# Retention in three bursts, its read-out turned by VectorE and a trip to DRAM

## The chip, the cores and the metric

The kernel runs on one core of a Trainium2 chip. The metric is the device time of one execution in microseconds (us). A core has five engines with a queue of instructions each, worked off in order: TensorE (PE in the profile, with its weight loads as PEld), VectorE (DVE), ScalarE (ACT), GpSimd (POOL) and SyncE (SP, which here only issues transfers). ACT and POOL issue transfers too. An instruction waits in its queue for semaphores that others raise, and whatever stands behind it waits as well.

## The reference, cut to what matters

Two layers, 512 positions, 1024 channels, float32. Each layer has a token mixer with three parallel branches (RWKV-7, retention, a gated spatial unit), merged by sigmoid gates, and then a gated MLP.

```python
p_rw, p_ret, p_sg, gate_logits = jnp.split(h @ w_in[l], in_cuts, axis=-1)
y_rw, y_ret, y_sg = rwkv7_branch(p_rw, ...), retention_branch(p_ret, cos, sin), sgu_branch(p_sg, ...)
proj = jnp.einsum('bsgc,gcd->bsgd', jnp.stack([y_rw, y_ret, y_sg], axis=2), w_branch[l])
x = x + jnp.sum(jax.nn.sigmoid(gate_logits...) * proj, axis=2) @ w_out[l]

# retention_branch: 4 chunks of 128 positions, 4 heads, q and k of 64, v of 128 channels
scores = jnp.einsum('bhnid,bhnjd->bhnij', qc, kc) * decay_in
inner = jnp.einsum('bhnij,bhnje->bhnie', scores, vc)
cross = jnp.einsum('bhnid,nbhde,hi->bhnie', qc, R_prev, q_dec)     # R_prev: running states
y = inner + cross
y = y * lax.rsqrt(jnp.mean(y * y, axis=-1, keepdims=True) + EPS)
return y.reshape(B, S, RET_V_WIDTH) * jax.nn.silu(g)
```

## The kernel before

Activations are kept with channels on the partitions (128) and positions along the row (512). A product is made of float32r halves: a raw weight tile of 128x512 (`wr`, three buffers) is loaded by SP (L123), cast on ACT to a high half (`sh` or `wh`, L136), the remainder is made on VectorE (`sl` or `wl`, L137), and for each 128 input channels TensorE does three wide matmuls (L153) into a PSUM accumulator (`acc`, four buffers). A raw buffer is free once its `sl` is made. `unit` works ahead by a few tiles. The inputs of a product are split in the same way by `split` (`hi` on ACT L145, `lo` on VectorE L146).

A scheduler sets the order inside each engine's queue from the order of the code; what is marked `keep_in_program_order` (called `po`) isn't moved against other marked instructions of its engine. What is shown below as the order of a queue is its result.

The string `SEQ` writes out the second half of the mixer, a letter a step:
- `0`, `1`, `2`: one of the eight merges of a branch (0 RWKV, 1 retention, 2 spatial gating). `merge` loads the gate (`gth`, issued by POOL) that an earlier stage left in DRAM, makes a product of four weight blocks (12 wide matmuls), multiplies gate and accumulator on VectorE and adds it to the sum.
- `H`: `ret_heads` loads the turned queries and keys (`qF`, `kF`) and copies halves of them and of the values to the other half of the partitions (`qS`, `vs`).
- `G`: `sgu_out`, a group of the spatial gating: four matmuls of 128x128 and two VectorE passes (`sgm`), then `split`. `U`: one block of its first factor.
- `S`: `ret_row(read, score)`, a burst of small matmuls of the retention. Five of them: the first makes the scores of chunk 0, the next three read chunk 0, 1, 2 out and make the scores of the next chunk, the last reads chunk 3. Two call `ret_states` (running states `R`). A read-out gives `X` in PSUM, with positions on the partitions. ACT squares it and sums (`rsq`, `rss`), VectorE multiplies by the gate (in place of `vt`, the tile `yg`), POOL raises the mean to -0.5 (`rrr`), ACT scales by that.
- `Y`: `ret_out` turns the four scaled tiles to channels on the partitions, by 16 TensorE transposes into PSUM and a `split` from there.

`to_dram` is an older helper: VectorE transposes within 32x32 blocks, and four transfers of 64 KB put the blocks in place in a DRAM tile (`tn`), in pieces of 128 bytes. The RWKV read-out and the queries and keys go this way, issued by POOL. Tiles come from pools: `u` (31 buffers of 128x512), `r` (16), `f` (39), `sm` (four PSUM banks).

## Time and profile before

| what | value |
|---|---|
| time, three runs | 1702.79, 1702.88, 1703.18 us; median 1702.88 |
| the profiled execution | 1702.28 us; span 1700.6 us; granted TensorE clock 0.999 |
| wide matmuls of the weights x hi/lo halves (the three groups `sh`, `sl`) | 432.3, 431.6, 431.1 us busy |
| ACT's cast of weights, VectorE's remainder (`sh`, `sl`) | 235.1 us, 263.4 us busy |
| TensorE's 32 transposes (16 a layer) | 271 to 273 ns each, between 407.0 and 1252.5 us |
| transfers | 214.20 MB, mean 126 GB/s |

The span is the time from the first to the last instruction of the profiled execution. A row of a timeline gives the start, the duration, engine, line, operation, output and inputs, shapes and the count of what was merged into the row; in brackets stands the idle time ahead of it and who ended that. Matmuls are pipelined, so the distance of two starts is the cost, not the duration. A float32 matmul of small tiles shows as two records.

### The profile page before, as it was taken

Reading aid. Unit: us, or ns where it says so; the run is one execution under the profiler, and the core shown is the slowest. Engines: PE = TensorE matmul, PEld = TensorE weight load, DVE = VectorE, ACT = ScalarE, POOL = GpSimd, SP = SyncE. Lnnn points to the kernel's source line nnn. Section 1 sums busy time; section 2 is a strip of 40 time slices with the busy share of each in tenths; the row PEclk is TensorE's granted clock in tenths of the full one; section 3 lists DMA queues with packets and bytes.
Section 4 is the critical chain, followed back from the end, with each engine's and each line's share of the span. In section 5 each row is a group of like instructions: output and inputs, shape, how many; then the busy total and the mean of one; then the engine's idle time right before and its main releaser. Section 6 shows DMA issues by size and latency. Waiting matters only on the chain.

```text
span 1700.6 us, 28356 instructions
## 1 busy us (share of the span) xinstructions
PE 1692.3 (100%) x10564; PEld 1390.6 (82%) x10564; DVE 1141.6 (67%) x2032; ACT 765.9 (45%) x1341; POOL 245.4 (14%) x326
## 2 busy tenths in 40 slices
PE   9999999999999999999999999999999999999998
PEld 7888877888888888888888888778888888888887
DVE  7887856567569777653367786564765798876432
ACT  7564433535355444333255634345343554443322
POOL 1122235114100000000011203441141000000010
PEclk9999999999999999999999999999999999999999
DMA  5334566446443333243332346555364454432531
GB/s 175 91 101 151 147 151 152 141 130 194 137 149 100 96 97 99 69 119 110 115 113 80 112 142 155 148 141 161 108 210 141 132 138 123 124 107 68 155 100 55
DMA packets 151337, 214.20 MB, mean 126 GB/s; under 512 B 48416, under 2 KB 57248, under 8 KB 151200
## 3 DMA queue, kind: packets, MB, share of 16 engines
q1 hardware_dynamic: 129552, 171.62, 34.2%
q0 software_dynamic: 9600, 21.77, 4.9%
q10 hardware_dynamic: 12048, 19.00, 3.4%
q8 instruction: 83, 1.36, 0.3%
q14 instruction: 54, 0.44, 0.1%
HBM read 181.92 MB, written 23.07 MB: 121 GB/s over the span
## 4 chain that ended last, share of the span: by engine, by line
PE 99%; DMA 0%; ACT 0%; DVE 0%; issue 0%
PE acc L153 88%; PE sm L153 4%; PE sm L647 2%; PE acc L287 1%; PE sm L561 1%; PE sm L915 1%; PE acc L1009 0%; PE sm L524 0%; PE sm L523 0%; DMA g<-pcols 0%; PE sm L898 0%; PE sm L959 0%; PE sm L805 0%; PE sm L795 0%; PE sm L578 0%; PE sm L579 0%
## 5 line engine op out<-in xcount | busy, mean ns | idle before, releaser
L153 PE MATMUL acc<-lo,sh 128*128 128x512 f32 x1108 | 432.3, 390 | 0.0
L153 PE MATMUL acc<-hi,sh 128*128 128x512 f32 x1108 | 431.6, 390 | 0.0
L153 PE MATMUL acc<-hi,sl 128*128 128x512 f32 x1108 | 431.1, 389 | 0.0
L136 ACT CAST sh<-wr 128x512 fp32r<-128x512 f32 (+1 forms) x385 | 235.1, 615 | 380.2 <-PE acc L153 263.4
L137 DVE TENSOR_TENSOR sl<-wr,sh 128x512 fp32r<-128x512 f32 (+1 forms) x385 | 263.4, 687 | 170.5 <-ACT sh L136 104.8
L153 PEld LDWEIGHTS acc<-lo,sh 128*128 128x128 f32 x1108 | 208.0, 188 | 44.1 <-issue 0.7
L153 PEld LDWEIGHTS acc<-hi,sl 128*128 128x128 f32 x1108 | 208.0, 188 | 43.7 <-issue 0.3
L153 PEld LDWEIGHTS acc<-hi,sh 128*128 128x128 f32 x1108 | 208.0, 188 | 42.9 <-issue 0.2
L136 ACT CAST wh<-wr 128x512 fp32r<-128x512 f32 x194 | 120.2, 620 | 227.9 <-PE acc L153 209.2
L153 PE MATMUL acc<-lo,wh 128*128 128x512 f32 x556 | 219.4, 395 | 0.0
L153 PE MATMUL acc<-hi,wl 128*128 128x512 f32 x556 | 217.0, 390 | 0.0
L153 PE MATMUL acc<-hi,wh 128*128 128x512 f32 x556 | 216.6, 390 | 0.0
L137 DVE TENSOR_TENSOR wl<-wr,wh 128x512 fp32r<-128x512 f32 x195 | 138.9, 712 | 111.6 <-ACT wh L136 104.7
L153 PEld LDWEIGHTS acc<-hi,wl 128*128 128x128 f32 x556 | 104.4, 188 | 22.6 <-issue 0.7
L153 PEld LDWEIGHTS acc<-lo,wh 128*128 128x128 f32 x556 | 104.3, 188 | 22.6 <-issue 0.3
L153 PEld LDWEIGHTS acc<-hi,wh 128*128 128x128 f32 x556 | 104.4, 188 | 20.9
L153 PE MATMUL acc<-ah,sh 128*128 128x512 f32 x352 | 108.3, 389 | 0.0
L1077 DVE TENSOR_TENSOR fu<-acc,rsF 128x512 f32<-128x512 f32 x88 | 60.5, 689 | 62.3 <-PE acc L153 62.3
L1079 ACT ACTIVATE cv<-fu,pc 128x512 f32<-128x512 f32 x88 | 71.6, 816 | 50.4 <-DVE fu L1077 47.5
L153 PE MATMUL acc<-wl,hi 128*128 128x512 f32 x192 | 78.0, 406 | 0.0
L1080 DVE SCALAR_TENSOR_TENSOR cv<-fu,pc,cv 128x511 f32<-128x511 f32 x88 | 65.4, 746 | 18.6 <-ACT cv L1079 18.6
L153 PEld LDWEIGHTS acc<-ah,sh 128*128 128x128 f32 x352 | 66.1, 188 | 13.7
(335 smaller groups left out, 2450.1 us busy)
## 6 DMA issues: line engine op xcount, KB each, us to landing
wr<-wall SPq DMA_DIRECT2D x480, 256.0 KB, 2.7
gd<-gth ACTq DMA_DIRECT2D x48, 256.0 KB, 3.3
gth<-gd POOLq DMA_DIRECT2D x48, 256.0 KB, 3.3
wr<-wdt SPq DMA_DIRECT2D x44, 256.0 KB, 2.7
wr<-wdn SPq DMA_DIRECT2D x40, 256.0 KB, 2.7
x<-xT SPq DMA_DIRECT2D x8, 256.0 KB, 4.7
tn<-ysq POOLq DMA_DIRECT2D x32, 64.0 KB, 3.3
tab<-rot ACTq DMA_DIRECT2D x8, 256.0 KB, 3.9
```

Of the source, the lines that this page charges most:

```text
L136: self.kept((high or self.nc.scalar.copy)(hi[:, :n], raw[:, :n]))
L137: self.kept(self.nc.vector.tensor_tensor(lo[:, :n], raw[:, :n], hi[:, :n], op=SUB))
L153: i = self.nc.tensor.matmul(*x, **y, **kw)
L287: po(self.nc.tensor.matmul(pss[j], w[:, j * 128:j * 128 + 128], x, start=k == n == 0, stop=k == 7 and n == 2))
L561: i = T.matmul(pK[hv[1 - h], j, :], bk[hv[h], c, 1, :], x[hv[h], c, :], start=True, stop=True)
L647: po(T.matmul(o, l, r, start=start, stop=True, skip_group_check=True))
L915: po(T.matmul(o, lhsT, rhs, start=new[b][q], stop=stop, skip_group_check=True))
L1077: V.tensor_tensor(u, ps, self.rsF, op=MUL)
L1079: A.activation(t, u, AF.Identity, scale=self.p("cw2", j), bias=self.p("cb", j))
L1080: V.scalar_tensor_tensor(t[:, 1:], u[:, :511], self.p("cw1", j), t[:, 1:], op0=MUL, op1=ADD)
```

## The change

- `SEQ` has three bursts instead of five, with the merges and gating groups around them in another order, and nine merges now stand between the last burst and the first retention merge.
- `ret_row(read)`: the first burst makes the scores of all four chunks and the first four states; the second reads chunks 0 and 1 out and makes the other states; the third reads chunks 2 and 3. Squares, gate multiplies and scalings come for two chunks at a time; the power on POOL has eight columns instead of four.
- Each scaled tile goes through `to_dram`, now issued by SP, and `ret_out` loads four tiles (`yF`) from DRAM and splits them. The 16 transposes of TensorE are gone.
- `ret_heads` loads `qF`, `kF` of the first heads and then of the second. The gates of branches 1 and 2 come from pool `u` instead of `f`.

```diff
--- before.py
+++ after.py
@@ -22,7 +22,7 @@
 RWC, RETC, SGC = 1792, 1536, 1024
 NU, NR, NFP = 31, 16, 39
 FILL = (35, 2, 1)
-SEQ = "0 H 0 0 G G S U S U G S 0 G S 0 0 S 2 2 0 0 Y 2 2 1 2 1 2 1 2 1 2 1 1 1 1"
+SEQ = "0 H 0 0 0 G G S U U G S 0 G S 0 0 2 2 0 2 2 2 Y 2 1 2 1 2 1 1 1 1 1 1"
 NRAW = 3
 START = "z0 w0 z1 w1 z2 w2 z3 s0 z4 s1 w3 z5 s2 s3 w4 z6 s4 w5 z7 s5 s6 w6 s7 w7"
 AHEAD = {None: 2, "p": 4, "r": 3, "f": 3, "u": 5}
@@ -380,10 +380,10 @@
         yrw, ysg, mg, out, m2 = self.yrw, [], [], [], 0
         self.pool = "r"
         rest = self.sgu_u(l, range(2, 4))
-        rows = iter([(None, 0), (0, 1), (1, 2), (2, 3), (3, None)])
+        rows = iter([None, 0, 2])
         for step in SEQ.split():
             if step == "S":
-                self.ret_row(*next(rows))
+                self.ret_row(next(rows))
             elif step == "G":
                 ysg.append(self.sgu_out(len(ysg)))
             elif step == "H":
@@ -868,7 +868,7 @@
 
         A, V, T, po = self.nc.scalar, self.nc.vector, self.nc.tensor, self.tc.keep_in_program_order
         self.qF, self.kF = [], []
-        for j in range(4):
+        for j in (0, 2, 1, 3):
             t = self.r((128, 4, 128), n="qF" if j < 2 else "kF")
             self.nc.sync.dma_start(t.rearrange("p c t -> p (c t)"), self.qk[128 * j:128 * j + 128, :])
             (self.qF if j < 2 else self.kF).append(t)
@@ -903,61 +903,66 @@
             else:
                 V.tensor_tensor(self.Rs[n + 1], self.Rs[n], at(n), op=ADD)
 
-    def ret_row(self, read, score):
+    def ret_row(self, read):
 
 
         nc, V, A, T, po = self.nc, self.nc.vector, self.nc.scalar, self.nc.tensor, self.tc.keep_in_program_order
         hv = [slice(0, 64), slice(64, 128)]
         X, new = [self.sm((128, 4, 128)) for _ in range(2)], [[True, True], [True, True]]
-        hd = [(j, p, h) for j in range(2) for p in range(2) for h in range(2)]
+        hd = [(j, p, h) for j in range(2) for p in range(2) for h in (1, 0)]
 
         def mm(b, q, o, lhsT, rhs, stop=True):
             po(T.matmul(o, lhsT, rhs, start=new[b][q], stop=stop, skip_group_check=True))
             new[b][q] = False
 
-        if read is not None:
-            v, g = self.vt[read], self.yg[read]
-            for j, p, h in [(j, p, 1 - h) for j, p, h in hd]:
+        if read is None:
+            for c in range(NC):
+                for j, p, h in hd:
+                    ts = slice(64 * p, 64 * p + 64)
+                    mm(h, h ^ j, X[h][hv[h ^ j], c, ts], self.kF[j][hv[h], c, ts], self.qF[j][hv[h], c, ts])
+            self.ret_states(0, 4)
+            self.sc = [self.u((128, 8, 64), n="sc") for _ in range(2)]
+            for h in range(2):
+                V.tensor_tensor(self.sc[h], X[h].rearrange("q c (p t) -> q (c p) t", t=64), self.c("le64").unsqueeze(1).to_broadcast([128, 8, 64]), op=MUL)
+            return
+        cs = range(read, read + 2)
+        for c in cs:
+            for j, p, h in hd:
                 i, o = 2 * j + h, h ^ j
-                w = v[hv[p], 128 * i:128 * i + 128] if p == o else self.vs[read][hv[o], j, :]
-                mm(o, p, X[o][hv[p], j, :], self.sc[hv[o], h, p, :], w, read == p == 0)
+                w = self.vt[c][hv[p], 128 * i:128 * i + 128] if p == o else self.vs[c][hv[o], j, :]
+                mm(o, p, X[o][hv[p], 2 * (c - read) + j, :], self.sc[h][hv[o], 2 * c + p, :], w, c == p == 0)
+        for c in cs:
             for j, p, h in hd:
-                if read or p:
-                    o, ts = h ^ j, slice(128 * read + 64 * p, 128 * read + 64 * p + 64)
+                if c or p:
+                    o, ts = h ^ j, slice(128 * c + 64 * p, 128 * c + 64 * p + 64)
                     q = self.qS if j else self.qF[0].rearrange("p c t -> p (c t)")
-                    mm(o, p, X[o][hv[p], j, :], q[hv[o], ts], self.Rs[2 * read + p][hv[o], j, :])
-        if score is not None:
-            for j, p, h in hd:
-                ts = slice(64 * p, 64 * p + 64)
-                mm(h, h ^ j, X[h][hv[h ^ j], 2, ts], self.kF[j][hv[h], score, ts], self.qF[j][hv[h], score, ts])
-        if read is not None:
-            sq, ss = self.u((128, 4, 128), n="rsq"), self.small((128, 4), "rss")
+                    mm(o, p, X[o][hv[p], 2 * (c - read) + j, :], q[hv[o], ts], self.Rs[2 * c + p][hv[o], j, :])
+        if read == 0:
+            self.ret_states(4, 7)
+        ss = self.small((128, 2, 4), "rss")
+        for c in cs:
+            sq, g = self.u((128, 4, 128), n="rsq"), self.yg[c]
             for i in range(4):
-                A.activation(sq[:, i, :], X[i % 2 ^ i // 2][:, i // 2, :], AF.Square, accum_out=ss[:, i:i + 1])
+                A.activation(sq[:, i, :], X[i % 2 ^ i // 2][:, 2 * (c - read) + i // 2, :], AF.Square, accum_out=ss[:, c - read, i:i + 1])
             for o in range(2):
-                V.tensor_tensor(self.heads(g, o), X[o][:, 0:2, :], self.heads(g, o), op=MUL)
-        if score is not None:
-            sc = self.u((128, 2, 2, 64), n="sc")
-            for h in range(2):
-                V.tensor_tensor(sc[:, h], X[h][:, 2, :].rearrange("q (p t) -> q p t", t=64), self.c("le64").unsqueeze(1).to_broadcast([128, 2, 64]), op=MUL)
-            self.sc = sc
-            if score < 2:
-                self.ret_states(4 * score, 4 + 3 * score)
-        if read is not None:
-            V.tensor_scalar(ss, ss, 4.0 / 128, 4e-6, op0=MUL, op1=ADD)
-            rr = self.small((128, 4), "rrr")
-            nc.gpsimd.tensor_tensor(rr, ss, self.c("mhalf")[:, 0:4], op=POW)
+                V.tensor_tensor(self.heads(g, o), X[o][:, 2 * (c - read):2 * (c - read) + 2, :], self.heads(g, o), op=MUL)
+        V.tensor_scalar(ss, ss, 4.0 / 128, 4e-6, op0=MUL, op1=ADD)
+        rr = self.small((128, 2, 4), "rrr")
+        nc.gpsimd.tensor_tensor(rr, ss, self.c("mhalf")[:, 0:8].rearrange("p (c i) -> p c i", i=4), op=POW)
+        if read == 0:
+            self.yd = self.turned()
+        for c in cs:
             for i in range(4):
-                o = g[:, 128 * i:128 * i + 128]
-                A.activation(o, o, AF.Copy, scale=rr[:, i:i + 1])
+                o = self.yg[c][:, 128 * i:128 * i + 128]
+                A.activation(o, o, AF.Copy, scale=rr[:, c - read, i:i + 1])
+            self.to_dram(self.u(n="yz"), self.yg[c], self.yd, c, nc.sync)
 
     def ret_out(self):
         out = []
         for h in range(4):
-            pt = self.sm()
-            for c in range(NC):
-                self.tc.keep_in_program_order(self.nc.tensor.transpose(pt[:, c * 128:c * 128 + 128], self.yg[c][:, h * 128:h * 128 + 128], self.c("ident")))
-            out.append(self.split(pt, self.f))
+            t = self.u(n="yF")
+            self.nc.sync.dma_start(t, self.yd[128 * h:128 * h + 128, :])
+            out.append(self.split(t, self.f))
         return out
 
 
@@ -1017,7 +1022,7 @@
     def merge(self, l, br, m, y, sum=None, add=None):
 
         nc = self.nc
-        t = self.f(n="gth")
+        t = (self.u if br else self.f)(n="gth")
         nc.gpsimd.dma_start(t, self.gd[br, m])
         ps = self.acc()
         self.matF(ps, ("wall", l, 58 + br * 4 + m // 2, m % 2 * 512), y)
```

What the scheduler makes of it, at three places of layer 0. First SP's queue from the second burst on. Before (weight loads `wr`, and the first input of the output projection, `xi`):

```order
L123 DMA wr_824_4452<-wall 128x512
L123 DMA wr_839_4530<-wall 128x512
L123 DMA wr_844_4552<-wall 128x512
L123 DMA wr_854_4607<-wall 128x512
L123 DMA wr_859_4630<-wall 128x512
L123 DMA wr_864_4653<-wall 128x512
L123 DMA wr_869_4675<-wall 128x512
L123 DMA wr_886_4733<-wall 128x512
L1036 DMA xi_971_5086<-xT 128x512
```

After, with the DRAM writes of the turned read-outs (`yz` to `tn`, four a tile, x4 and x2 are merged rows):

```order
L123 DMA wr_827_4484<-wall 128x512
L123 DMA wr_844_4590<-wall 128x512
L442 DMA tn_822_4460<-yz_823_4465 32x16x32 x4
L442 DMA tn_822_4460<-yz_824_4475 32x16x32 x2
L123 DMA wr_849_4612<-wall 128x512
L442 DMA tn_822_4460<-yz_824_4475 32x16x32
L123 DMA wr_854_4634<-wall 128x512
L123 DMA wr_859_4657<-wall 128x512
L442 DMA tn_822_4460<-yz_824_4475 32x16x32
L123 DMA wr_864_4680<-wall 128x512
L123 DMA wr_869_4702<-wall 128x512
L123 DMA wr_874_4725<-wall 128x512
```

Eight writes for the first two chunks now stand among the weight loads, six of them ahead of `wr_849`.

Second, ACT's queue. Before, around the read-out of chunk 2 (`hi_829` is the cast of the last gating group):

```order
L952 ACTIVATE vt_652_3737<-vt_652_3737,rrr_821_4443 128x128 x4
L136 CAST sh_840_4532<-wr_808_4372 128x512
L136 CAST sh_845_4554<-wr_824_4452 128x512
L136 CAST sh_855_4609<-wr_839_4530 128x512
L145 CAST hi_829_4479<-sgm_828_4476 128x512
L936 ACTIVATE rsq_833_4509,rss_834_4510<-sm_831_4483 128x128 x2
L936 ACTIVATE rsq_833_4509,rss_834_4510<-sm_832_4484 128x128 x2
L136 CAST sh_860_4632<-wr_844_4552 128x512
L136 CAST sh_865_4655<-wr_854_4607 128x512
L136 CAST sh_870_4677<-wr_859_4630 128x512
L136 CAST sh_887_4735<-wr_864_4653 128x512
```

After, from the scalings of the first two chunks to the squares of the last two (`hi_832` is the cast of the last gating group):

```order
L957 ACTIVATE vt_650_3732<-vt_650_3732,rrr_821_4458 128x128 x4
L957 ACTIVATE vt_652_3737<-vt_652_3737,rrr_821_4458 128x128 x4
L136 CAST sh_845_4592<-wr_806_4362 128x512
L136 CAST sh_850_4614<-wr_827_4484 128x512
L136 CAST sh_855_4636<-wr_844_4590 128x512
L136 CAST sh_860_4659<-wr_849_4612 128x512
L145 CAST hi_832_4511<-sgm_831_4508 128x512
L136 CAST sh_865_4682<-wr_854_4634 128x512
L946 ACTIVATE rsq_837_4550,rss_836_4549<-sm_834_4515 128x128
L946 ACTIVATE rsq_837_4550,rss_836_4549<-sm_835_4516 128x128 x2
L946 ACTIVATE rsq_837_4550,rss_836_4549<-sm_834_4515 128x128
L946 ACTIVATE rsq_838_4557,rss_836_4549<-sm_835_4516 128x128 x2
```

The scalings of two chunks and the casts of five weight tiles now stand between the second burst's squares and the third's, and the cast of `wr_849` stands ahead of `hi_832`.

Third, VectorE's queue. Before, from the last gating group's pass to the gate multiply of chunk 2:

```order
L1011 SCALAR_TENSOR_TENSOR sgm_828_4476<-acc_827_4471,pc_45_181,bs_532_2912 128x512
L137 TENSOR_TENSOR sl_841_4533<-wr_808_4372,sh_840_4532 128x512
L1013 TENSOR_TENSOR sgm_828_4476<-sgm_828_4476,sgu_811_4390 128x512
L137 TENSOR_TENSOR sl_846_4555<-wr_824_4452,sh_845_4554 128x512
L146 TENSOR_TENSOR lo_830_4480<-sgm_828_4476,hi_829_4479 128x512
L137 TENSOR_TENSOR sl_856_4610<-wr_839_4530,sh_855_4609 128x512
L938 TENSOR_TENSOR vt_654_3742<-sm_831_4483,vt_654_3742 128x2x128
L942 TENSOR_TENSOR sc_835_4517<-sm_831_4483,con_78 128x128
L938 TENSOR_TENSOR vt_654_3742<-sm_832_4484,vt_654_3742 128x256
```

After, from the two 32x32 transposes of the first read-out to the remainder of the last gating group (`lo_833`), which is an input of all merges of branch 2:

```order
L440 STREAM_TRANSPOSE yz_823_4465<-vt_650_3732 128x512
L440 STREAM_TRANSPOSE yz_824_4475<-vt_652_3737 128x512
L1029 SCALAR_TENSOR_TENSOR gth_825_4481<-gth_825_4481,acc_826_4483 128x512
L137 TENSOR_TENSOR sl_846_4593<-wr_806_4362,sh_845_4592 128x512
L1016 SCALAR_TENSOR_TENSOR sgm_831_4508<-acc_830_4503,pc_45_181,bs_532_2912 128x512
L137 TENSOR_TENSOR sl_851_4615<-wr_827_4484,sh_850_4614 128x512
L137 TENSOR_TENSOR sl_856_4637<-wr_844_4590,sh_855_4636 128x512
L1018 TENSOR_TENSOR sgm_831_4508<-sgm_831_4508,sgu_809_4380 128x512
L137 TENSOR_TENSOR sl_861_4660<-wr_849_4612,sh_860_4659 128x512
L146 TENSOR_TENSOR lo_833_4512<-sgm_831_4508,hi_832_4511 128x512
```

Two transposes that wait for ACT's scalings now stand ahead of a merge's multiply, the weight splits and the gating group.

## Prediction

> **What bounds the kernel now.** I read the page's head and the shares of the chain that ended last, then who made TensorE wait, then TensorE's timeline in the stretch that the change rewrites (360 to 412 us in layer 0; layer 1 runs the same rows again), then the other engines there.
>
> ```profile
> span 1700.6 us, 28356 instructions
> PE 1692.3 (100%) x10564; PEld 1390.6 (82%) x10564; DVE 1141.6 (67%) x2032; ACT 765.9 (45%) x1341; POOL 245.4 (14%) x326
> PE 99%; DMA 0%; ACT 0%; DVE 0%; issue 0%
> ```
>
> TensorE's waits, all of them, and one stretch of the chain (start, us, what):
>
> ```profile
> PE acc L308 <- DVE rst L305: 1.5, 1, 1.5
> PE acc L287 <- DVE wh L136: 0.4, 1, 0.4
> ...
> 409.10 95.34 PE acc L153 x420
> ```
>
> TensorE waits for nobody after the start: its instructions are the time. A wide matmul (128x512) costs 95.34 / 420 = 0.227 us from start to start. So work taken from TensorE counts in full, and any new wait of TensorE counts in full too; work moved to other engines counts only if it makes TensorE wait.
>
> **What leaves TensorE.** Starts in its timeline:
>
> ```profile
> 374.83 0.32 PE L915 MATMUL sm<-vs,sc 64*64 64x128 f32 x1
> 377.02 0.50 PE L153 MATMUL acc<-lo,sh 128*128 128x512 f32 x1
> ...
> 381.91 1.05 PE L1009 MATMUL acc<-ws,sgv 128*128 128x128 f32 x8
> 382.89 0.32 PE L915 MATMUL sm<-vs,sc 64*64 64x128 f32 x1
> ...
> 384.22 0.50 PE L153 MATMUL acc<-lo,sh 128*128 128x512 f32 x1
> 384.56 0.40 PE L153 MATMUL acc<-hi,sh 128*128 128x512 f32 x1
> ...
> 387.11 1.05 PE L1009 MATMUL acc<-ws,sgv 128*128 128x128 f32 x8
> 387.92 0.48 PE L153 MATMUL acc<-lo,sh 128*128 128x512 f32 x1
> ...
> 407.19 1.91 PE L959 MATMUL sm<-con,vt 128*128 128x128 f32 x16
> 408.85 0.48 PE L153 MATMUL acc<-lo,sh 128*128 128x512 f32 x1
> 409.17 0.39 PE L153 MATMUL acc<-hi,sh 128*128 128x512 f32 x1
> ```
>
> - The 16 transposes of `ret_out`: 408.85 - 407.19 = 1.66 us a layer.
> - The first wide matmul after a run of small ones costs 0.34 us (384.56 - 384.22) or 0.32, not 0.227; with slower neighbours a return costs some 0.2 (the 12 wide matmuls from 384.22 to 387.11 take 2.89 where 12 x 0.227 is 2.72). Before, a layer's stretch returns eight times (the gating pair, five bursts, of which one has a gating group ahead, a lone gating group, the transposes); after, three times. 5 x 0.2 = 1.0 us.
> - Scores, read-outs and states are the same matmuls in other batches, so they cost what they cost before; the pair of heads inside a batch is taken in the other order, which changes no count.
>
> Gain 2.7 us a layer, 5.4 in all, if TensorE still waits for nobody.
>
> **What the new order asks of the others.** Rows of ACT, VectorE and POOL:
>
> ```profile
> 384.65 0.62 ACT L145 CAST hi<-sgm 128x512 fp32r<-128x512 f32 x1 [0.69 <-DVE sgm L1013]
> 385.18 0.27 ACT L936 ACTIVATE rsq<-sm 128x128 f32<-128x128 f32 x1
> 385.44 0.27 ACT L936 ACTIVATE rsq<-sm 128x128 f32<-128x128 f32 x1
> ...
> 388.71 1.28 ACT L952 ACTIVATE vt<-vt,rrr 128x128 f32<-128x128 f32 x4 [0.78 <-POOL rrr L949]
> ...
> 397.78 1.97 ACT L136 CAST sh<-wr 128x512 fp32r<-128x512 f32 x3 [2.70 <-DMA wr<-wall]
> ```
>
> ```profile
> 386.45 0.41 DVE L938 TENSOR_TENSOR vt<-sm,vt 128x256 f32<-128x256 f32 x1
> ...
> 387.08 0.69 DVE L137 TENSOR_TENSOR sl<-wr,sh 128x512 fp32r<-128x512 f32 x1
> 387.69 0.68 DVE L1024 SCALAR_TENSOR_TENSOR gth<-gth,acc 128x512 f32<-128x512 f32 x1
> ```
>
> ```profile
> L947 DVE TENSOR_SCALAR rss<-rss x8: 158/160/160, 378.4 to 1248.7; 128x4 f32<-128x4 f32 x8
> ```
>
> ```profile
> L717 POOL TENSOR_TENSOR rs<-s,con 128x8 f32<-128x8 f32 x8 | 13.3, 1665 | 58.2 <-DVE s L715 58.0
> ```
>
> ```profile
> L440 DVE STREAM_TRANSPOSE ysq<-y x8: 704/708/712, 238.1 to 1146.5; 128x512 f32<-128x512 f32 x8
> ```
>
> And the transfers (median us to landing; min/median/max ns of an issue; the wait of SP's queue):
>
> ```profile
> wr<-wall SPq DMA_DIRECT2D x480, 256.0 KB, 2.7
> tn<-ysq POOLq DMA_DIRECT2D x32, 64.0 KB, 3.3
> yF<-tn SPq DMA_DIRECT2D x8, 256.0 KB, 4.1
> xr<-xz SPq DMA_DIRECT2D x32, 64.0 KB, 2.1
> kF<-tn SPq DMA_DIRECT2D x4, 256.0 KB, 3.9
> ```
>
> ```profile
> L1054 SPq DMA_DIRECT2D xr<-xz x32: 325/426/478, 1360.4 to 1505.2; - x32
> ```
>
> ```profile
> L636 SPq DMA_DIRECT2D cs<-cs x64: 585/612/1897, 197.0 to 1108.6; - x64
> ```
>
> ```profile
> SPq L123 <- DVE sl L137: 772.2, 362, 18.9
> ```
>
> I follow the queues as the order shows them, in us from the first matmul of the second burst (the first with a read-out), and write down when each step is done. *TensorE without waits.* the burst takes 2.6 (the 2.19 from 374.83 to 377.02, plus 16 more small matmuls at 0.03 each: a burst of 48 took 384.22 - 382.89 = 1.33), a merge 2.9, the last gating group 1.0 (382.89 - 381.91), the third burst 1.8 (64/48 x 1.33): 8.3. Then 33 wide matmuls (7.5, and 0.2 for the return) lead to the first use of the fourth gating output (`lo_833`): TensorE is there at 16.0. Nine merges (24.5) lead to `lo_884`, the first retention merge: 33.0.
>
> *The chain on the others, second burst.* The square starts 2.3 after a burst that follows a gating group (385.18 - 382.89), here 2.7, as one split more stands ahead on VectorE. Two rounds, one a chunk, of four squares (0.26 each, 1.0) and two multiplies (0.41, some 0.5 beyond the squares); the second round's squares wait for the first round's multiplies, which read the same banks: until 5.8. The small scale on VectorE, 0.16; power on eight columns 1.67; eight scalings at 0.30 (1.28 for four), 2.4; with the hand-overs ACT is done at 10.3, the second 32x32 transpose (0.71) at 11.0. VectorE, which stood behind it, does a gate multiply and a split (0.6 each): 12.2. Only then is raw buffer `wr_806` free; SP meanwhile issued six of eight DRAM writes, at 0.43 each from 9.7 on (12.3). The weight load `wr_849` goes out at 12.3 and lands at 15.1 (2.7). ACT's queue has its cast ahead of the gating output's cast (0.62 each, 0.53 from start to start, 385.18 - 384.65): 15.7, 16.3. VectorE's queue has the same load's `sl` ahead of the gating output's `lo`: 16.4, 17.1; some eight hand-overs of 0.05 make it 17.5. **First wait: 17.5 - 16.0 = 1.5.**
>
> *Third burst.* Its squares stand behind the cast of `wr_854` as well (landed 15.9, cast until 16.8), though TensorE was done at 8.3. The same round: squares and multiplies 19.9, power 21.9, scalings 24.4, transposes 25.1; then two splits (1.2) and the multiply of `gth_852` (0.7) at 27.0, which frees the accumulator that TensorE, without waits, wants at 24.8 (the sixth merge's end). **Second wait: 27.2 - 24.8 = 2.4 in all, the 1.5 included.**
>
> *The trip to DRAM.* Eight writes and two weight loads on SP from 24.4: last one issued at 28.0, landed 30.1 (2.1, as the same engine's 64 KB writes) to 31.3 (3.3, POOL's); `yF` lands 2.7 to 4.1 later, cast and remainder 1.3: `lo_884` at 34.1 to 36.7 against 33.0, so 1.1 to 3.7 in all. The two cover each other: 2.4 to 3.7. I take 3.4, near the dear end, since ACT already waited 2.70 for a weight load here.
>
> The Trainium skill (DMA: Bandwidth & Descriptors, "Anatomy of one DMA") puts a DMA at about 2.0 us plus bytes over 436 GB/s, an estimate of 2.15 for 64 KB and 2.6 for 256 KB. `wr` agrees at 2.7; `tn` (3.3) and `yF` (4.1) do not. By it `lo_884` would be there at 34.0, the waits 2.4, and the slow rival below would lose half its chance.
>
> *Smaller edits.* The two loads of `kF`, and their first use on TensorE:
>
> ```profile
> 363.88 0.80 SPq L873 DMA_DIRECT2D kF<-tn  x2
> ```
>
> ```profile
> 369.88 0.47 PE L915 MATMUL sm<-qF,kF 64*64 64x64 f32 x16
> ```
>
> With `qF`/`kF` in another order the second pair waits for the same merge's end, but now only 12 wide matmuls (2.7) and two gating groups (387.92 - 387.11 = 0.81 each) lie between that and its first use, 4.4 against 6.0 before (363.88 to 369.88). Landing 3.9 plus two issues: between 0 and 0.6 of wait, taken as 0.3. The gates of branches 1 and 2 in the larger pool: nothing, the loads run ahead; but branch 2's five now stand on POOL behind the second power (21.9 + 3.3 = 25.2, used at 26.3): a cover of 1.1 us. The states' adds on VectorE end at 7.3, as the third burst reaches them: 0.
>
> **Sum.** A layer: -2.7 + 0.3 + 3.4 = +1.0; two layers +2.0. The profiled execution took 1702.28 us (span 1700.6, 1.7 around it); 1704.3 against it, and 1704.9 in terms of the median, which is 0.6 above it.
>
> **Rivals.**
> 1. *SP's queue decides: slower.* If a DRAM write in 128-byte pieces costs SP 0.61 (the `cs` row, also 128-byte pieces) rather than 0.43, six of them delay `wr_849` by 1.1, so the squares, and eight more the trip by 1.4: with landings of 3.3 and 4.1 that is 36.7 + 2.5 = 39.2, a wait of 6.2. A layer +3.8, in all +7.6: 1710.5. For it: SP's row of 772 us shows that loads are issued only as buffers come free. Against: SP's own writes to DRAM (0.43). It decides once the waits pass 4.4 a layer. 0.31.
>
> POOL's power on four columns:
>
> ```profile
> L949 POOL TENSOR_TENSOR rrr<-rss,con 128x4 f32<-128x4 f32 x8 | 9.6, 1204 | 57.9 <-DVE rss L947 57.9
> ```
>
> 2. *The waits are covered: faster.* If the scalings are done 1.5 to 2.5 us earlier, both waits vanish and -5.4 stands: 1697.5. For it: two powers at 1.2, as on four columns, instead of 1.67 give 0.9 to the second wait, and a round of squares that takes no turns another 1.0 each time. Against: the first wait has only one power and one round ahead of it, and three queues in a row must be quick, in both layers. 0.21.
> 3. *The array slows after a wait.* If it ran at half speed for as long as it stood (2.4 us at 0.454 a wide matmul), that is 1.2 a layer more: 1707.3. The trace has no idle stretch to show it; the granted clock (after PE, PEld, DVE, ACT, POOL) is full even in the first 8 us:
>
> ```profile
> 0.00:8.00 8.00, 6.09 (x17) 4.53 (x18) 3.25 (x6) 4.51 (x8) 0.20 (x4) 1.00 0.74 246
> ```
>
> 0.05. The Trainium skill (TensorE: Matmul & The Clock Gate, "Part 1: The HAM clock gate") says that about 3.4 us of idleness halves the clock; no wait forecast here is that long in one piece.
>
> **How the numbers follow.** The forecast has 0.43, rivals 1 and 3 together 0.36 (slower), rival 2 0.21 (faster). Within 0.2% means 3.4 us, about what a measurement can tell from no change. The likeliest gives 1704.9; its own range is 1700 to 1706 (waits of 1.3 to 4.3 a layer). To hold eight in ten, the range takes in the upper part of rival 2 and most of rival 1: 1698 to 1712.
>
> **What would show it.** TensorE's transposes gone and three returns a layer; an idle of 1 to 2 us on TensorE ended by VectorE's remainder (`lo` of `sgm`, L146) some 16 us after the second burst; a second ended by the gate multiply (L1029) or by `lo` of `yF`; ACT's squares of the third burst some 8 us after its matmuls; SP's `wr` loads standing behind `tn<-yz`. Wrong it would be if TensorE has no such idle (then faster), or if the wait for `yF` alone exceeds 3 us.

## The result, and the profile after

1721.49 us (median of four, 1720.29 to 1725.15) against 1703.03; ratio 1.0109, interval 1.0092 to 1.0127. The change makes the kernel 18.5 us slower; 1704.9 was forecast, with 1712.0 as the upper end. In e13 and e15 the profiled execution ran at a granted clock of 0.56 and 0.75, so their times below are the medians of the other executions, and no waits are read from their profiles.

The page's head and the shares of the chain that ended last, then TensorE's waits (total, times, longest):

```profile
span 1718.5 us, 28321 instructions
PE 1694.9 (99%) x10532; PEld 1390.6 (81%) x10532; DVE 1151.2 (67%) x2024; ACT 766.4 (45%) x1341; POOL 245.2 (14%) x322
PE 93%; DMA 2%; DVE 1%; ACT 1%; issue 1%; SPq 0%; POOL 0%; DVEq 0%; POOLq 0%; ACTq 0%
```

```profile
PE acc L153 <- DVE lo L146: 14.0, 7, 3.0
...
PE acc L287 <- ACT hi L211: 1.1, 1, 1.1
PE acc L153 <- DVE gth L1029: 0.5, 1, 0.5
```

Before, TensorE waited for nobody after the start. Now it waits eight more times, 14.5 us: seven times for remainders (`lo`) and once for a gate's multiply. TensorE's timeline around the two long waits of layer 0:

```profile
399.95 0.39 PE L153 MATMUL acc<-hi,sl 128*128 128x512 f32 x1
403.14 0.50 PE L153 MATMUL acc<-lo,sh 128*128 128x512 f32 x1 [2.80 <-DVE lo L146]
...
404.00 0.63 PE L153 MATMUL acc<-lo,sh 128*128 128x512 f32 x1
404.42 0.63 PE L153 MATMUL acc<-hi,sh 128*128 128x512 f32 x1
...
425.04 0.80 PE L153 MATMUL acc<-lo,sh 128*128 128x512 f32 x1 [2.96 <-DVE lo L146]
425.63 0.63 PE L153 MATMUL acc<-hi,sh 128*128 128x512 f32 x1
426.06 0.63 PE L153 MATMUL acc<-hi,sl 128*128 128x512 f32 x1
```

The first (2.80) is the last gating group's `lo`, the second (2.96) that of `yF`. Behind each the starts stand 0.42 apart instead of 0.227. Windows of 5 us say why: the granted clock (third column from the right) falls, and the share of the DMA engines (second from the right) stands at 0.81 to 1.04.

```profile
400.00:405.00 5.00, 2.20 (x8) 1.48 (x7) 2.67 (x5) 3.02 (x13) 0.00 (x0) 0.89 0.81 218
...
410.00:415.00 5.00, 5.00 (x24) 4.14 (x23) 4.54 (x8) 2.32 (x6) 2.60 (x4) 1.00 1.01 293
415.00:420.00 5.00, 5.00 (x24) 4.14 (x23) 1.37 (x3) 1.23 (x2) 1.68 (x3) 1.00 1.04 210
...
425.00:430.00 5.00, 4.96 (x12) 3.91 (x13) 2.58 (x4) 1.39 (x3) 2.10 (x5) 0.50 0.93 335
```

In both layers 28 wide matmuls stand some 0.42 apart, 5.9 us more than at 0.227. The balance: 14.5 of waits + 5.9 of half clock - 5.4 of forecast gain = 15.0, of the 17.9 between the spans. Another 0.7 is the kernel's start (L287: 1.1, before 0.4), and the step after a wait takes 0.34 instead of 0.23 (eight times, 0.9); some 1.3 stays unassigned.

What the other queues did there, SP, POOL, VectorE and ACT in turn:

```profile
393.42 4.66 SPq L442 DMA_DIRECT2D tn<-yz  x6
398.17 0.46 SPq L123 DMA_DIRECT2D wr<-wall  x1
...
410.37 2.24 SPq L442 DMA_DIRECT2D tn<-yz  x4
412.71 2.20 SPq L123 DMA_DIRECT2D wr<-wall  x1
...
415.96 1.65 SPq L442 DMA_DIRECT2D tn<-yz  x3
...
420.58 1.27 SPq L964 DMA_DIRECT2D yF<-tn  x3
```

```profile
391.30 2.19 POOL L1026 DMA_DIRECT2D gth<-gd  x4
...
420.83 4.26 POOL L1026 DMA_DIRECT2D gth<-gd  x8
```

```profile
395.88 0.69 DVE L1029 SCALAR_TENSOR_TENSOR gth<-gth,acc 128x512 f32<-128x512 f32 x1 [1.32 <-DMA gth<-gd]
```

```profile
401.14 0.62 ACT L136 CAST sh<-wr 128x512 fp32r<-128x512 f32 x1 [5.77 <-DMA wr<-wall]
...
423.64 0.62 ACT L145 CAST hi<-yF 128x512 fp32r<-128x512 f32 x1 [1.85 <-DMA yF<-tn]
...
427.12 0.62 ACT L145 CAST hi<-yF 128x512 fp32r<-128x512 f32 x1 [1.87 <-DMA yF<-tn]
...
430.72 0.62 ACT L145 CAST hi<-yF 128x512 fp32r<-128x512 f32 x1 [2.45 <-DMA yF<-tn]
```

The first six writes took SP 4.66 us, 0.78 each on the mean (one of them 1.71), not 0.43. The gate of the merge behind the second burst left POOL only at 391.3, behind the power, and VectorE stood for it, 1.32 us. And eight gate loads went out at 420.83 together with `yF`, whose four tiles came in over 7 us.

### The profile page after: what moved, and what is told of

It is laid out like the page before. It is cut to its first block, busy times and chain, and to the rows that moved or that the text cites. A ratio compares the mean times of both kernels' runs of the same rounds, so it can differ in the third digit from the quotient of the medians.

```text
span 1718.5 us, 28321 instructions
## 1 busy us (share of the span) xinstructions
PE 1694.9 (99%) x10532; PEld 1390.6 (81%) x10532; DVE 1151.2 (67%) x2024; ACT 766.4 (45%) x1341; POOL 245.2 (14%) x322
## 4 chain that ended last, share of the span: by engine, by line
PE 93%; DMA 2%; DVE 1%; ACT 1%; issue 1%; SPq 0%; POOL 0%; DVEq 0%; POOLq 0%; ACTq 0%
PE acc L153 84%; PE sm L153 4%; PE sm L647 2%; PE acc L287 1%; DMA yF<-tn 1%; DMA wr<-wall 1%; PE sm L561 1%; DVE sl L137 0%; ACT rsq L946 0%; ACT vt L957 0%; POOL rrr L951 0%; DMA gth<-gd 0%; DMA x<-xT 0%; SPq L442 0%; PE sm L524 0%
```

## The experiments

Theories: 1, the trip to DRAM costs nearly all (1a: by transfers that collide with gate loads; 1b: by SP's queue); 2, the three bursts cost; 3, rows of gate loads that POOL issues at once fill the DMA engines; 4, too few raw buffers; 5, a gate that is late behind POOL's power.

**e1_pe_turn: bursts with TensorE's transposes.** `ret_out` as before, and

```diff
-            self.yd = self.turned()
-            self.to_dram(self.u(n="yz"), self.yg[c], self.yd, c, nc.sync)
```

> Three bursts as changed, but the turned read-out by TensorE's 16 transposes a layer as before: no DRAM writes on SP, no yF. Theory 1 (the trip to DRAM costs nearly all: its writes stand among SP's weight loads, its reads come late): both waits ended by `lo` vanish but for under 1 us of the first; gain of the returns 1.0 a layer stays: 1701 to 1703.5. Theory 2 (the three bursts themselves cost: two chunks' squares, powers and scalings ahead of the gating cast on ACT): the first wait stays at 2 to 3 us a layer with its slow clock behind it: 1708 to 1712.

1713.61, ratio 1.0059 (1.0044 to 1.0074): 7.9 less than the whole change. So the trip is not all: theory 1 fails, and theory 2 has 10 us. But not as it said, since the first wait grew from 2.80 to 4.73. POOL's rows, and the landing of weight loads between 388 and 432 us (before 2.4/3.0/5.9):

```profile
391.61 4.29 POOL L1024 DMA_DIRECT2D gth<-gd  x8
396.36 5.74 POOL L1024 DMA_DIRECT2D gth<-gd  x9 [0.47 <-PE acc L153]
```

```profile
DMA to landing us min/median/max: 2.6/4.0/8.0
```

17 gate loads leave with hardly a pause, where the change had four and then five. Theory 3 was made from this.

**e2_gates_f: all gates from pool `f`.**

```diff
-        t = (self.u if br else self.f)(n="gth")
+        t = self.f(n="gth")
```

> As changed, but the gates of all branches come from pool f again. Theory 1a (transfers collide: the larger pool lets POOL issue eight gate loads in a row at 420.8 us, just as yF is loaded, and yF lands in 4.3 to 6.4 us): yF lands in about 3 us, the second to fourth yF waits vanish and the first shrinks: 1712 to 1716. Theory 1b (SP's queue: the writes stand behind weight loads that wait for raw buffers): within 2 us of the changed kernel, 1719.5 to 1722.

1722.62, ratio 1.0113 (1.0098 to 1.0128): no different from the whole change. Inside it is: the waits for `yF` shrank (0.4 us in layer 0 and 2.5 in layer 1, the way 1a said), the first wait became 5.6 us, since eight gates now left at 391.1, and TensorE waited 8.2 us for gate multiplies. Of these, 5.0 us fall near the ends of the layers, far from any power, and VectorE stood for no gate there. So the pool decides where the row of loads falls, and the sum came out the same; that is a balance of these parts, and no proof that the pool costs nothing.

**e3_tn_pool: the writes issued by POOL.**

```diff
-            self.to_dram(self.u(n="yz"), self.yg[c], self.yd, c, nc.sync)
+            self.to_dram(self.u(n="yz"), self.yg[c], self.yd, c, nc.gpsimd)
```

> As changed, but the DRAM writes of the read-out are issued by POOL instead of SP. Theory 1b (SP's queue): weight loads go out when their buffers come free, wr_849 some 4 us earlier, so the first wait vanishes, and the writes no longer stand behind weight loads, so yF some 3 us earlier: 1705 to 1711. Theory 1a (the 16 DMA engines are full, whoever issues): the 128-byte pieces take the same time and the gates the same place: 1717 to 1722.

1730.00, ratio 1.0156 (1.0141 to 1.0172). Slower than either theory said: at 0.65 us a write, eight held the gates behind them up to 399, and TensorE waited 8.5 us for gate multiplies and 6.9 in one piece for `yF`. It frees SP and blocks POOL in the same way.

**e4_y_late: all merges of branch 2 ahead of `Y`.**

```diff
-SEQ = "0 H 0 0 0 G G S U U G S 0 G S 0 0 2 2 0 2 2 2 Y 2 1 2 1 2 1 1 1 1 1 1"
+SEQ = "0 H 0 0 0 G G S U U G S 0 G S 0 0 2 2 0 2 2 2 2 2 2 Y 1 1 1 1 1 1 1 1"
```

> As changed, but the string has all eight merges of branch 2 ahead of Y, so the first use of yF comes three merges (8.2 us) later. All theories of the trip: the yF waits (about 7 us a layer with the slow clock behind them) vanish, the first wait stays: 1706 to 1710. Were the reads of yF slowed by the gates wherever they stand, some 2 us a layer of it would stay: 1710 to 1713.

1717.10, ratio 1.0080 (1.0063 to 1.0097): 4.4 less where 11 to 15 was expected, or 8 to 11 were the reads slowed by the gates. `yF`'s loads went out at 422.0, eight gates at 423.6 beside them; 3.5 us of waits for `yF` stayed in layer 0 and 3.2 in layer 1.

**e5_pe_paced and e6_all_paced: gates loaded by SP, one ahead of each weight load.** The list of gates is worked off three merges ahead, both kinds of load in the order of the code:

```diff
-        nc.gpsimd.dma_start(t, self.gd[br, m])
+        while self.glist and len(self.gq) <= 3:
+            b, n = self.glist.pop(0)
+            g = ...
+            self.tc.keep_in_program_order(nc.sync.dma_start(g, self.gd[b, n]))
+            self.gq.append(g)
+        t = self.gq.pop(0)
```

> Three bursts with TensorE's transposes, and the gates loaded by SP instead of POOL, one ahead of each merge's weight load (three merges ahead of use). Theory 3 (a convoy of gate loads: POOL holds them back behind the two long powers, then issues 8 and 9 in a row, which fill the DMA engines, and a weight load lands in 6 us instead of 2.7): no stretch of the first 30 us after the second burst is at full DMA share, weight loads land in about 3 us, the first wait falls from 4.7 to about 1, no slow clock: 1702 to 1705. Theory 2 (the two chunks' chain on ACT and VectorE itself makes the weight tile late): the wait stays at 2.5 us or more a layer: 1708 to 1713.

1708.25, ratio 1.0029 (1.0018 to 1.0040): 5.4 less than e1. By the time alone this lies at the edge of theory 2, but the wait that theory 2 named is gone. The stretch of the first wait has none left in either layer; windows and the landing of weight loads (394 to 403 us):

```profile
400.00:405.00 5.00, 5.00 (x24) 4.14 (x23) 2.94 (x7) 3.15 (x15) 1.64 (x1) 1.00 0.31 87
```

```profile
DMA to landing us min/median/max: 2.6/2.8/3.1
```

That is theory 3's mark. What remained (4.3 us with 3.0 of half clock at 420 us, 1.5 in layer 1) is the split of the transposes: ACT made it behind two casts that waited 2.5 and 0.7 us for their weight loads. e17 comes back to this.

> The whole change, gates loaded by SP, one ahead of each merge's weight load. Theory 3: yF and the weight loads land in 3 us, of the waits some 1 us of the first and 1 to 2 us of yF's stay, since the writes still stand on SP: 1703 to 1709. If the 128-byte writes alone fill the DMA engines, the six issues still take 0.7 us each, and both waits stay near 3 us with the slow clock: 1714 to 1721.

1721.54, ratio 1.0111 (1.0094 to 1.0128): a miss. With gates and weights in fixed order the writes came to stand eight in a row ahead of the weight loads, SP stood up to 12.0 us for the transposes, and TensorE waited 8.8 and 5.9 us for a cast. One thing it shows: SP's eight writes, now with no gate load beside them, at 0.52 us each.

```profile
393.88 4.15 SPq L449 DMA_DIRECT2D tn<-yz  x8
```

**e7_before_gates_u and e8_before_trip: one part each in the kernel before.** The first is one line:

```diff
-        t = self.f(n="gth")
+        t = (self.u if br else self.f)(n="gth")
```

> The kernel before with one edit of the change, the gates of branches 1 and 2 from the larger pool. POOL's queue then has 14 gate loads in a row behind the fourth power instead of six and three with adds between. Theory 3: where those 14 (3.6 MB) go at some 390 GB/s they fill the DMA engines for 9 us, weight loads land late, and TensorE waits 1 to 4 us a layer: 1705 to 1711. If a convoy of gates does nothing while weight loads run ahead: 1702 to 1704.

1718.49, ratio 1.0090 (1.0075 to 1.0105): this edit alone costs 15.6 us, more than theory 3 put, and in part by another path. POOL, and TensorE's waits:

```profile
398.82 4.30 POOL L1021 DMA_DIRECT2D gth<-gd  x8
...
408.85 1.04 POOL L949 TENSOR_TENSOR rrr<-rss,con 128x4 f32<-128x4 f32 x1
```

```profile
PE sm L959 <- ACT vt L952: 10.5, 2, 5.6
```

The last burst's power stands behind 14 gate loads. It ran at 408.85, 3.5 us later than the same power before (405.36 there): that is the other path. The larger part came after it: ACT's scalings ran only at 418.5, behind casts of weight tiles that landed in 4.2 us (median, before 3.0) while the DMA engines' share was 0.93 to 1.03, as theory 3 has it. TensorE waited for the scalings with its transposes.

> The kernel before (five bursts, its order of steps) with one edit of the change, the read-out turned by VectorE and by SP's DRAM writes and yF loads. Y stands four merges and a burst nearer to the last read-out than in the change, so yF must come late: TensorE waits 6 to 10 us a layer there, less 1.66 for the transposes: 1712 to 1724. Were writes and reads hidden: 1700.

Its edits are `ret_out` and the two lines of e1, the other way round. 1721.99, ratio 1.0112 (1.0097 to 1.0127): 19 us, as expected; TensorE waits 8.4 us a layer for the first `yF`.

**e9_bursts_alone: e1 with e2's line.** Bursts and string of the change, nothing else.

> The three bursts and their order of steps alone: TensorE's transposes as before, all gates from pool f as before. POOL's queue has nine gate loads in a row between the two powers (17 where the gates came from pool u). Theory 3 (rows of gate loads make the weight loads late): shorter rows, so less than the 1713.6 of the run with the larger pool: 1706 to 1710. Theory 4 (three raw buffers: while ACT holds two chunks' squares and scalings for 7 us, no weight tile is cast, no raw buffer comes free, and loads go out late whatever the gates do): the first wait stays near 4 us a layer: 1710 to 1715.

1714.58, ratio 1.0065 (1.0048 to 1.0081). VectorE behind the second burst, and TensorE's waits:

```profile
395.72 0.69 DVE L1027 SCALAR_TENSOR_TENSOR gth<-gth,acc 128x512 f32<-128x512 f32 x1 [4.99 <-DMA gth<-gd]
```

```profile
PE acc L153 <- DVE gth L1027: 6.3, 4, 1.9
PE acc L153 <- DVE lo L146: 3.8, 1, 3.8
```

The bursts alone cost 11.6, by theory 4's number. VectorE's row gave theory 5: the gate left POOL behind the power, VectorE stood 5.0 us, and the weight remainders, hence the raw buffers, behind it. Three of the four waits for a gate's multiply (453.9, 458.7 and 1302.3 us) lie near the ends of the layers, where VectorE stood for no gate; there the multiply stood in its queue behind a weight remainder whose cast waited for TensorE.

> The run before in this call, with four raw buffers for weight tiles instead of three. Theory 4: one load more is on its way during ACT's stretch of squares and scalings, so the weight tile that TensorE waited for is there some 2.7 us earlier; the waits fall to under 2 us a layer and the slow clock goes: 1702 to 1705. Theory 3: rows of gate loads still fill the DMA engines, a fourth buffer only adds to the queue: within 2 us of the run before.

1712.53, ratio 1.0056 (1.0041 to 1.0071); against e9's 1714.58 a gain of 2.1, not 10. The first wait did go (3.8 to 0.3), but the waits for gate multiplies grew from 6.3 to 8.3. And **e11_all_raw4**, the same in the whole change:

> The whole change with four raw buffers. Theory 4: the first wait (2.5 to 3 us a layer and its slow clock) goes, yF's stays: 1711 to 1715. Theory 3: 1718 to 1722.

1724.42, ratio 1.0126 (1.0111 to 1.0141): not faster. In layer 0 the first wait shrank to 0.4, with 2.1 for a gate's multiply behind it; the wait for `yF` grew to 8.8. Theory 4 holds for the first wait, not for the time.

**e12_spread_raw4: another string, four raw buffers.**

```diff
+SEQ = "0 H 0 0 G G S U U G G S 0 0 0 S 0 0 2 2 2 2 2 2 2 2 Y 1 1 1 1 1 1 1 1"
+NRAW = 4
```

> The whole change with four raw buffers and another string: all four gating groups ahead of the second burst, three merges between it and the third, all branch 2 merges ahead of Y, so ten merges (27 us) lie between the last burst and the first use of yF, and no gating output hangs on a late weight tile. If the waits come from the order of steps (a short way from each burst to what needs its helpers), they all go and the gain of 2.7 us a layer shows: 1697 to 1700. If DMA engines full of gates and 128-byte pieces cost wherever they stand: 1706 to 1715.

1710.21, ratio 1.0039 (1.0024 to 1.0054). The first wait is gone, and `yF` still 2.1 us late in each layer, the DMA engines full from 405 to 430 us; the first burst, one merge nearer to `H`, waited 1.7 and 3.2 us for `kF`.

**e13_bursts_gate and e14_all_gate: each gate's load written one merge earlier**, in e9 and in the whole change, on POOL as before. Five gates instead of four then stand ahead of the first power.

> The bursts alone (TensorE's transposes, gates from pool f) with each gate's load written one merge earlier: on POOL exactly one more gate, that of the merge behind the second burst, now stands ahead of the first long power; the row of nine behind it stays. Theory 5 (a late gate: POOL sits 26.9 us in the power's wait, the gate lands at 395.7, VectorE stands 5.0 us at its multiply with the weight remainders behind it, so a raw buffer comes free late and TensorE waits 3.8): VectorE doesn't stand there, the first wait falls by 1.5 to 3 us in layer 0 and goes in layer 1: 1707 to 1711. Theory 3 (the row of gates fills the DMA engines, whatever the first gate does): 1712 to 1715.

1705.46, ratio 1.0016 (1.0006 to 1.0025): 2.7 of the bursts' 11.6 us are left. Where its waits are is read from e18 below, which differs in the place of `Y` alone: there the 6.3 us of waits for gate multiplies are gone, and the first wait (3.0 instead of 3.8) is not. So the 8.9 us aren't all one gate behind POOL's power. Near the ends of the layers VectorE stood for no gate in e9, and why an earlier load ended those waits is open.

> The whole change with each gate's load written one merge earlier, so that five instead of four gates stand ahead of the first power on POOL. Theory 5: VectorE's stop for the gate was 1.32 us here, behind the transposes: the first wait falls by about 1.3 us a layer, the slow clock behind it with it: 1716 to 1719. If SP's six writes (0.78 us each) decide the first wait: 1720 to 1722.

1718.34, ratio 1.0092 (1.0077 to 1.0107): 3.2 less than the whole change. VectorE's multiply at 394.87 has no wait ahead of it, and the first wait is 1.74 and 1.28 instead of 2.80 and 2.45. But theory 5 isn't the reason. SP's six writes, here in layer 0 and in the change in layer 1:

```profile
393.80 3.64 SPq L448 DMA_DIRECT2D tn<-yz  x6
```

```profile
1246.12 4.33 SPq L442 DMA_DIRECT2D tn<-yz  x6
```

With three gate loads behind the power instead of four, the six writes take 3.64 and 3.19 us instead of 4.66 and 4.33, and the weight load behind them leaves sooner. In the change its raw buffer was free by 397.17, VectorE's stop included, and SP came to it only at 398.17; in layer 1 VectorE didn't stand at all (its multiply at 1247.19 has no wait), and TensorE still waited 2.45. So at the first wait of the whole change SP's writes decide, and theory 5 isn't on the path; the time expected for that case, 1720 to 1722, missed as well.

**e15_spread_paced**: the whole change with string `0 H 0 0 0 G G S U U G G S 0 0 S 0 0 2 2 2 2 2 2 2 2 Y 1 1 1 1 1 1 1 1`, e5's gates, e3's writes. **e16_spread_pe**: the same string and gates, TensorE's transposes.

> The whole change with other places for what hangs on it: three merges ahead of the first burst, all gating groups ahead of the second, ten merges between the last burst and yF's first use, gates loaded by SP one ahead of each weight load, the 128-byte writes issued by POOL. If the waits come from queues (late gate, writes among weight loads, rows of gates), none is left but for under 1 us of yF: 1697 to 1700. If the 128-byte pieces fill the DMA engines so that weight loads and yF are late anyway: 1703 to 1712.

1708.78, ratio 1.0037 (1.0022 to 1.0051). Where its waits are stays open. Beside e16, which leaves out the trip alone, the trip costs some 3 us here.

> Three bursts with TensorE's transposes, the same string, gates loaded by SP: no DRAM trip at all. If three bursts have room for their helpers in this order, no wait is left, and the gain of five returns (1.0 us a layer) shows: 1700 to 1702. If ACT's 7 us of squares and scalings alone starve the weight loads: 1704 to 1709.

1705.86, ratio 1.0017 (1.0007 to 1.0027); the profiled execution, 1711.04, was the longest of ten. TensorE waits in it once a layer, 3.0 and 2.4 us. ACT there:

```profile
427.00 0.62 ACT L136 CAST sh<-wr 128x512 fp32r<-128x512 f32 x1 [1.70 <-PE sm L969]
427.52 2.04 ACT L145 CAST hi<-sm 128x512 fp32r<-128x512 f32 x4
```

The transposes are followed at once by the merge that needs their split (`Y 1`); the kernel before has two merges between.

**e17_spread_pe_y**: e16 with `2 2 2 2 2 2 Y 2 2 1 1 ...`; **e18_bursts_gate_y**: e13 with `2 2 0 2 2 Y 2 2 1 2 ...`.

> As e16_spread_pe, but the TensorE transposes of the read-out (Y) stand two merges of branch 2 earlier, as in the kernel before, so that ACT's and VectorE's split of them has 5.4 us of cover instead of none. If e16's only waits (3.0 and 2.4 us, and 1.6 of slow clock) were the split without cover: all go, 1700 to 1701.5, and the bursts' gain of five returns a layer shows. If ACT's stretch starves the weight loads wherever the waits show: 1703 to 1706.

1701.57 (eleven runs), ratio 0.9994 (0.9985 to 1.0003). All of TensorE's waits:

```profile
PE acc L308 <- DVE rst L305: 1.5, 1, 1.5
PE acc L287 <- DVE wh L136: 1.0, 1, 1.0
PE acc L153 <- DVE sl L137: 0.2, 1, 0.2
```

Before, these were 1.9 us. Three bursts cost nothing where their helpers have time. Their gain is 1.2 us, not to be told from none. In this string the gates were also issued by SP, so it isn't the places alone that differ from the change.

> As e13_bursts_gate, with Y (TensorE's transposes) one merge earlier. Theory 5 as there: VectorE doesn't stand at the gate's multiply behind the second burst, no wait over 1.5 us follows in the 20 us behind that burst in layer 0, none in layer 1. Where the rest of e13's 3 us over the kernel before was the split's short cover: 1701 to 1704; where it was the row of gates: 1704.5 to 1707.

1706.63, ratio 1.0020 (1.0011 to 1.0028). No wait in layer 1; in layer 0 one of 3.0 us with 3.0 of half clock. VectorE, POOL, ACT, and a window:

```profile
391.00 0.68 DVE L1038 SCALAR_TENSOR_TENSOR gth<-gth,acc 128x512 f32<-128x512 f32 x1
```

```profile
391.64 4.30 POOL L1033 DMA_DIRECT2D gth<-gd  x8
```

```profile
401.72 0.62 ACT L136 CAST sh<-wr 128x512 fp32r<-128x512 f32 x1 [6.00 <-DMA wr<-wall]
```

```profile
395.00:400.00 5.00, 5.00 (x24) 4.13 (x23) 2.86 (x5) 0.72 (x2) 0.95 (x2) 1.00 0.96 328
```

The early gate does free VectorE (391.0 instead of e9's 395.7), and the weight load leaves at 395.43 instead of 397.04. But the row of eight gates keeps the DMA engines full, that load lands after 6.2 us instead of 5.0, and ACT waits 6.0. So in the bursts alone the late gate was worth 0.8 us of this wait (3.8 to 3.0) and the row the rest; e5, which takes both causes away, has no wait at this place. A wait of 3.0 us in layer 0 wasn't expected here: 1.5 was the most.

## Why the prediction was wrong

- *Sum.* +2.0 was forecast, and the spans differ by 17.9. Of the 15.9 between, 7.1 are waits (14.5 instead of the 7.4 in the sum), 5.9 are half clock, which stood in no term of the sum, and 2.9 are the start, the steps after waits and what stays unassigned.
- *Bound and gain: right.* Waits of TensorE count in full, and it was waits that came. The transposes left. The returns were put at 2.0 for both layers; e17, in which only they remain, has 1.2 (2.6 down to a loss of 0.5 by its interval), or some 1.6 if the 0.8 us of waits that its profile has beyond the kernel before are set aside.
- *First wait: right place and queues, one term too small.* `lo` of the last gating group, behind `wr_849`: 2.80 and 2.45 instead of 1.5. From the second burst's start (384.01) the scalings ended at 9.8 (forecast 10.3) and the second transpose at 10.6 (11.0), TensorE was there at 16.3 (16.0). Then came the term that was mis-sized. SP's writes took 0.78 each, not 0.43, and `wr_849` left at 14.2 instead of 12.3. The 0.43 was from a row (`xr`) in another stretch, with pieces of 512 bytes. VectorE also stood 1.32 us for a gate that I had put at nothing, but that wasn't on the path: the raw buffer was free at 13.2, before SP was done.
- *The gates: the step that failed.* "The gates of branches 1 and 2 in the larger pool: nothing, the loads run ahead." I looked only at when buffers come free and at one gate's cover behind the second power. POOL issues in order. A gate behind a power leaves when the power ends (late: 391.30 in the change, and VectorE's 5.0 us in e9), and those behind it then leave in a row as long as there are buffers, while the DMA engines move 328 to 365 GB/s (e1, e18), or hold up the next power (e7, where this one line costs 15.6 us). In the kernel before, four shorter powers a layer broke the row up: six gates at most. What a row costs depends on what runs beside it: SP's writes took 0.61 us each beside three gates and 0.78 beside four, a weight load 6.2 us beside eight, `yF` 4.3 and 6.4 at the median beside eight. The pool isn't the whole of it: with the smaller one (e2) the time was the same.
- *The trip: mechanism right, size off.* `lo` of the first `yF` was ready at 41.0, not 34.1 to 36.7. The scalings ended at 26.7 (24.4); the last write left SP at 33.6 (28.0), since weight loads between the writes waited for raw buffers; writes landed in 4.5 (2.1 to 3.3), and `yF` beside eight gates in 3.0 to 5.6 in layer 0, 6.4 at the median in layer 1. Each landing was bounded by rows from a quieter stretch. In all, the waits for `yF` are 3.5 us in layer 0 and 5.3 in layer 1, over the 3 us that the prediction named as a sign of being wrong. The estimates of 2.15 and 2.6 us that I had worked out from the Trainium skill (DMA: Bandwidth & Descriptors, "Anatomy of one DMA", where the fit is for transfers that GpSimd issues) are further off. The second wait, for `gth_852`'s accumulator, didn't show on its own: TensorE, held by the first, came there later.
- *`kF`: right.* No wait for it (0 to 0.6, taken as 0.3).
- *Rivals taken as exclusive.* Rival 1 (SP's queue, 0.31) and rival 3 (half clock, 0.05) came together, and the first sets off the second: 5.9 us of half clock, against 2.4 in rival 3, and 14.5 of waits. My 1712.0 took in most of one rival alone.

## What to carry to other kernels

An in-order queue that both computes and loads turns a longer wait into late loads first and into a burst of loads after; look at what stands behind each waiting instruction, the loads above all, and count how many leave at once when it ends. Where a change gives loads more buffers, ask which transfers then run together, and take landing times from a stretch as full as the new one. Three bursts could be had for nothing, but only once gates, gating groups and the read-out's turn had been given their places (e17); even then the gain is that of the ten returns alone, 1.2 us, because TensorE had no wait to lose.

## What the runs showed of the hardware

- Half clock follows waits shorter than I had thought. In e4 a wait of 1.90 us was followed by it; one of 2.45 (layer 1 of the change) was not; every wait of wide matmuls from 2.77 us on (e3) had one that began during it or no later than 1.53 us after its end. A slow stretch in the clock's records lasted 3.41 us or two to three times that, the longer ones partly inside the wait. Mostly 6 to 8 wide matmuls then stood 0.42 apart, 14 at the most (e5 and e18), which cost 1.0 to 1.6 us mostly and 3.0 at the most. The Trainium skill (TensorE: Matmul & The Clock Gate, "Part 1: The HAM clock gate") has a free-running window of 3413 ns. The length of the slow stretches agrees with it, and that waits of about 2 us sometimes hit and sometimes miss fits it; the table's "after ≥1 idle window (~3.4µs)" doesn't agree, as no run needed 3.4 us of idleness.
- A DMA issue is no constant. SP's 64 KB writes in 128-byte pieces took, on the mean, 0.52 us each with no gate load beside them (e6), 0.61 with three (e14), 0.78 with four (the change) and 0.92 with eight (e2), and up to 2.24 for a single one (e2).
